# Feed-forward of a two-layer encoder trunk: both down blocks of a pair stand between its seventh and its third product

## The chip, the cores and the metric

The kernel runs on one core of a Trainium2 chip. The metric is the device time of one execution in microseconds (us). A difference of 0.2% is 2.9 us here.

## What is computed

Two layers over 512 tokens of width 1024, all in float32. Each layer has a mixer (attention in layer 0, an mLSTM in layer 1), a cross-attention to a memory, and a gated feed-forward; the change lies in the feed-forward of both layers:

```
def conv_ffn(xn, w_up, conv_w, conv_b, w_down):
    h = causal_depthwise_conv(xn @ w_up, conv_w) + conv_b     # 1024 -> 2 x 2816, 3 taps
    g, u = jnp.split(h, 2, axis=-1)
    return (jax.nn.gelu(g) * u) @ w_down                      # 2816 -> 1024
...
x = x + conv_ffn(rms_norm(x, ffn_norm[layer]), ffn_w_up[layer], ffn_conv_w[layer], ffn_conv_b[layer], ffn_w_down[layer])
```

## The kernel before

The 2816 columns of each half are worked through in 22 "pairs" p of 128 columns of g and the 128 columns of u that belong to them. Activations lie transposed, so that a product has a 128x128 piece of a weight as the stationary operand and 256 or 512 tokens as the moving one. For precision every float32 operand is split into a high and a low part, and each product is done as three matmuls (high x high, low x high, high x low: lines 292, 293, 294, in `mm3`). Splitting a weight costs ScalarE (ACT) one cast to the high part and VectorE (DVE) one subtraction to the low part (line 283, `sub`).

Pair 0 goes the plain way (`plain`). Pairs 1 to 21 (`seven`) use a scheme of seven half-size products instead of eight, each of 12 matmuls with 256 moving columns, in the order p1, p5, p6, p2, p7, p3, p4 of the code (the "seventh" product is p7, the "third" p3, the "last" p4 in the code's names). Their stationary operands are sums of weight blocks:

- f3 (raw tile `raw`) serves p1 and p2, f1 (raw tile `sa`, summed by a POOL transfer that accumulates) serves p5 and p7; both are 1024 columns wide and lie in three rotating slots `wh`/`wl`, which they share with the down blocks.
- `s2` serves p6, `s4` serves p3, `a22` serves p4: 512 columns each, one slot each. Both `s2` and `s4` are made from the tile `sb` (lines 1768 and 1774).

Between the products, results are passed on: after p1 ACT seeds a second PSUM bank with its negative (line 1801, "v"); after p5 ACT copies a bank to `u5`, after p6 to `u2` (line 1805). p7 writes on to the bank that `u2` is copied from, so it waits for that copy. After p7 DVE forms one quarter of the result (`hs<-acc,u`, line 1808), after p3 another (`hs<-s,u`, line 1808), after p2 and p4 ACT copies the other two (lines 1818 and 1825). When all four are there, DVE scales them by the norm (line 1831), and a "tail" follows: two convolution starts on ACT (1684), four taps on DVE (1691), GELU on ACT (1699), the product with u on DVE (1701), and the split of the activation (1705 on ACT, `al` on DVE).

The products with `w_down` ("down blocks") run over chunks of 2 or 4 pairs, 8 blocks per chunk. A block is 6 or 12 matmuls with 512 moving columns into a bank `w`; its weight comes through the tile `dr` (two slots; cast on line 1568, subtraction on 283). For most blocks ACT first seeds the bank with the sum so far (1598) and copies it back afterwards (1855). Where a block is followed by a 256-column product, the last 128 columns of its low part are written with an offset, which makes its subtraction two instructions. From pair 3 on, a call of `fill()` in the code of a pair takes the next block from a queue and puts it at that place.

The order on every engine is set by a list scheduler (`Sched`) with the given due times and costs, and from there it is fixed: each engine works its own queue in order and waits at the head of it.

Of the kernel before, what the change touches and what calls it, by code (L numbers as in the profile page):

```python
# [66 lines left out]
class Plan:  # L67
# [11 lines left out]
    def add(self, fn, dur=0.0, deps=(), prio=None, take=(), free=(), chain=(), pre=(), after=0.0, order=(), load=(), st=None):  # L79
        it = Item(fn, dur, [d for d in deps if d is not None], len(self.items) if prio is None else prio, take, free, chain, pre, after, order, load, st)  # L80
        it.n = len(self.items)
        self.items.append(it)
        return it
# [154 lines left out]
class Builder:  # L238
# [22 lines left out]
    def bank(self, tag):  # L261
        tag, bufs = BANKS[tag]
        return self.til(self.aux, tag, bufs=bufs)
# [1257 lines left out]
    def ffn_steps(self, layer, mp):  # L1521
# [15 lines left out]
        def pe(dur, fn, deps, take=(), free=()):  # L1537
            clock[0] += dur
            return add("PE", dur, fn, deps, clock[0] - dur, take, free, 0.2)
# [198 lines left out]
        def seven(p, fill):  # L1738
# [41 lines left out]
            def product(s, c, xh, xl, bank, first):  # L1780

                for k in range(4):
                    w = slice(c + k * P, c + (k + 1) * P)
                    self.mm3(st[bank][:, :256], s["wh"][:, w], s["wl"][:, w], xh(k), xl(k), first and k == 0, k == 3, True)
# [22 lines left out]
            def less(out, a, b):  # L1807
                tt_(out=out(), in0=a(), in1=b(), op=ALU.subtract)
# [10 lines left out]
            p7 = pe(n, lambda: product(f1, 0, *T3, "Y", False), [u2, p5], (), [("h", f1)])  # L1819
            c22 = add("DVE", 0.34, lambda: less(hs(1, 1), bank("Y"), lambda: st["u5"][:]), [p7, u5, get], clock[0], (), [("u5", bu5)])  # L1820
            fill()
            p3 = pe(n, lambda: product(s4, 0, *X(1, 1), "R", False), [u5, w4], (), [("s4", s4)])
            c12 = add("DVE", 0.34, lambda: less(hs(0, 1), bank("R"), lambda: st["u2"][:]), [p3, u2, get], clock[0], (), [("s", br), ("u2", bu2)])
            p4 = pe(n, lambda: product(a22, 0, *T4, "Y", False), [c22, w22], (), [("a22", a22)])
# [6 lines left out]
                tt_(out=h, in0=h, in1=self.rb.unsqueeze(1).to_broadcast([P, 2, 512]), op=ALU.mult)  # L1831

            m = add("DVE", 1.14, scaled, [c11, c22, c21, c12, normed], clock[0] + 2.0)
            fill()
            tail(p, st, [[m], [m]], clock[0] + 3.0)


# [3 lines left out]
        def down(c, m, steps=1):  # L1841
            first, nk = CHUNKS[c]
            onto = (self.x[m], [xadded[m]]) if c < LAST and (c, m) not in ((0, 0), (0, 1)) else None
            d, last = block(
                t[f"down{c}"][layer, m], nk, lambda k: tuple(a[:] for a in acts[first + k]), clock[0], "w", [acted[first + k] for k in range(nk)], steps,
                "dr" if c < LAST else "raw", OFF, onto,
            )
            last.block, d["step"] = d, 16
            if m == 7:
                for k in range(nk):  # L1850
                    joined([last], last.prio, [("act", acted[first + k].st)])
            if onto is None:
                e = add("DVE", 0.6, lambda: self.xadd(m, d["ps"]), [last, xadded[m], *formed], clock[0] + 3.0, (), [("w", d)])
            else:
                e = add("ACT", act(512), lambda: nc.scalar.copy(self.x[m][:], d["ps"][:]), [last, *formed], clock[0] + 1.0, (), [("w", d)])
            xadded[m] = e
            return e

        def fill():
            nonlocal queue  # L1860
            if queue:
                down(*queue.pop(0))
# [468 lines left out]
```

## Time and profile before

| | us |
|---|---|
| median of 3 runs | 1452.01 (1451.99 to 1452.08) |
| the profiled execution, its own time | 1451.94 |
| its span in the trace | 1450.1 |
| TensorE (PE) busy | 1435.6 |
| DVE busy | 1226.5 |
| ACT busy | 1009.8 |
| POOL busy | 74.8 |

The time of the execution and its span differ by 1.84 us, which lie around the span. The feed-forward of layer 0 stands at about 415 to 739 us of the span, that of layer 1 at about 1114 to 1436. In a row of the timeline the first number is the start in us from the span's start, the second the duration, then engine, line, operation, output and inputs; in brackets the idle time before it and what ended it. Instructions of one engine overlap a little: what counts in a queue is the distance from start to start.

### The profile page before, as it was taken

Reading aid. Unit: us, or ns where it says so; the run is one execution under the profiler, and the core shown is the slowest. Engines: PE = TensorE matmul, PEld = TensorE weight load, DVE = VectorE, ACT = ScalarE, POOL = GpSimd, SP = SyncE. Lnnn points to the kernel's source line nnn. Section 1 sums busy time; section 2 is a strip of 40 time slices with the busy share of each in tenths; the row PEclk is TensorE's granted clock in tenths of the full one; section 3 lists DMA queues with packets and bytes.
Section 4 is the critical chain, followed back from the end, with each engine's and each line's share of the span. In section 5 each row is a group of like instructions: output and inputs, shape, how many; then the busy total and the mean of one; then the engine's idle time right before and its main releaser. Section 6 shows DMA issues by size and latency. Waiting matters only on the chain.

```text
span 1450.1 us, 24100 instructions
## 1 busy us (share of the span) xinstructions
PE 1435.6 (99%) x8971; PEld 1274.2 (88%) x8971; DVE 1226.5 (85%) x2199; ACT 1009.8 (70%) x1830; POOL 74.8 (5%) x116
## 2 busy tenths in 40 slices
PE   9999999999999999999999999999999999999998
PEld 7888788998889999999888788889988999999997
DVE  7789987877899988888689888887779999888875
ACT  7689766655678777777657676566566787777775
POOL 0001120000000000000000100000000000000000
PEclk9999999999999999999999999999999999999999
DMA  5222337652246665552233322656313666655312
GB/s 199 89 74 73 110 119 214 178 167 87 95 118 170 183 164 158 155 166 68 66 128 106 121 94 98 188 144 181 132 52 113 165 182 175 153 163 159 101 52 95
DMA packets 73367, 190.38 MB, mean 131 GB/s; under 512 B 8081, under 2 KB 10258, under 8 KB 73250
## 3 DMA queue, kind: packets, MB, share of 16 engines
q1 hardware_dynamic: 65474, 162.30, 33.6%
q0 software_dynamic: 7200, 26.22, 10.6%
q8 instruction: 70, 1.15, 0.3%
q14 instruction: 47, 0.39, 0.1%
q10 hardware_dynamic: 576, 0.33, 0.1%
HBM read 186.69 MB, written 2.13 MB: 130 GB/s over the span
## 4 chain that ended last, share of the span: by engine, by line
PE 80%; DVE 12%; ACT 4%; issue 2%; DMA 1%; POOL 0%; SPq 0%; DVEq 0%; ACTq 0%; POOLq 0%
PE acc L292 14%; PE acc L293 14%; PE acc L294 14%; PE w L294 6%; PE w L292 6%; PE w L293 6%; PE s L294 3%; PE s L292 3%; PE s L293 3%; DVE wl L283 3%; PE acc L353 2%; PE acc L355 2%; PE acc L354 2%; DVE c L1691 1%; DVE x L774 1%
## 5 line engine op out<-in xcount | busy, mean ns | idle before, releaser
L283 DVE TENSOR_TENSOR wl<-raw,wh 128x1024 fp32r<-128x1024 f32 (+2 forms) x181 | 209.4, 1157 | 37.5 <-ACT wh L286 29.0
L292 PE MATMUL acc<-xh,wh 128*128 128x256 f32 (+1 forms) x624 | 206.9, 332 | 0.2 <-ACT v L1932 0.2
L294 PE MATMUL acc<-xh,wl 128*128 128x256 f32 (+1 forms) x624 | 205.6, 329 | 0.1
L293 PE MATMUL acc<-xl,wh 128*128 128x256 f32 (+1 forms) x624 | 205.5, 329 | 0.0
L286 ACT CAST wh<-raw 128x1024 fp32r<-128x1024 f32 (+1 forms) x123 | 124.8, 1019 | 73.3 <-PE acc L293 35.7
L1691 DVE SCALAR_TENSOR_TENSOR c<-hs,vec,c 128x512 f32<-128x512 f32 x176 | 131.0, 747 | 14.6 <-ACT c L1684 12.6
L292 PEld LDWEIGHTS acc<-xh,wh 128*128 128x128 f32 x624 | 117.2, 188 | 12.8 <-ACT v L1932 0.9
L293 PEld LDWEIGHTS acc<-xl,wh 128*128 128x128 f32 x624 | 117.2, 188 | 12.2
L294 PEld LDWEIGHTS acc<-xh,wl 128*128 128x128 f32 x624 | 117.1, 188 | 12.1 <-DVE wl L283 0.7
L294 PE MATMUL w<-ah,wl 128*128 128x512 f32 x320 | 125.3, 392 | 0.0
L293 PE MATMUL w<-al,wh 128*128 128x512 f32 x320 | 124.8, 390 | 0.0
L292 PE MATMUL w<-ah,wh 128*128 128x512 f32 x320 | 124.8, 390 | 0.0
L1684 ACT ACTIVATE c<-hs,vec 128x512 f32<-128x512 f32 x88 | 71.2, 816 | 13.8 <-DVE hs L1831 7.4
L283 DVE TENSOR_TENSOR wl<-sa,wh 128x1024 fp32r<-128x1024 f32 x52 | 63.5, 1221 | 20.2 <-ACT wh L1762 18.5
L1568 ACT CAST wh<-dr 128x512 fp32r<-128x512 f32 (+1 forms) x80 | 46.0, 575 | 42.1 <-PE w L293 35.3
L294 PEld LDWEIGHTS w<-ah,wl 128*128 128x128 f32 x320 | 60.1, 188 | 12.7
L1762 ACT CAST wh<-sa 128x1024 fp32r<-128x1024 f32 x42 | 44.0, 1049 | 36.3 <-PE w L293 33.3
L292 PEld LDWEIGHTS w<-ah,wh 128*128 128x128 f32 x320 | 60.1, 188 | 10.3 <-ACT w L1598 0.2
L293 PEld LDWEIGHTS w<-al,wh 128*128 128x128 f32 x320 | 60.1, 188 | 10.1
L283 DVE TENSOR_TENSOR wl<-dr,wh 128x128 fp32r<-128x128 f32 (+3 forms) x148 | 55.6, 410 | 9.4 <-ACT wh L1568 9.3
L1747 POOL DMA_DIRECT2D sa<-in_up_dram x42 | 35.9, 855 | 514.8 <-DVE hs L1831 209.7
L283 DVE TENSOR_TENSOR s<-sb,s 128x512 fp32r<-128x512 f32 x88 | 60.2, 685 | 2.2
(571 smaller groups left out, 4656.1 us busy)
## 6 DMA issues: line engine op xcount, KB each, us to landing
raw<-in_up_dram SPq DMA_DIRECT2D x46, 512.0 KB, 3.2
sa<-in_up_dram SPq DMA_DIRECT2D x42, 512.0 KB, 3.4
sa<-in_up_dram POOLq DMA_DIRECT2D x42, 512.0 KB, 5.8
dr<-in_down_dram SPq DMA_DIRECT2D x64, 256.0 KB, 2.6
ra<-in_up_dram SPq DMA_DIRECT2D x42, 256.0 KB, 2.8
raw<-in_xk_dram SPq DMA_DIRECT2D x16, 512.0 KB, 3.3
raw<-in_wo_dram SPq DMA_DIRECT2D x16, 512.0 KB, 3.8
raw<-in_xv_dram SPq DMA_DIRECT2D x16, 512.0 KB, 3.3
```

What stands on the lines that cost most here:

```text
L283: self.nc.vector.tensor_tensor(out=lo, in0=v, in1=hi.bitcast(F32), op=ALU.subtract)
L286: self.nc.scalar.copy(hi, v)
L292: mm(out, wh, xh, start=first, stop=False, skip_group_check=parts)
L293: mm(out, wh, xl, start=False, stop=False, skip_group_check=parts)
L294: mm(out, wl, xh, start=False, stop=last, skip_group_check=parts)
L353: mm(ps, xh[k][:, ts], wh[:, ws], start=(k == 0), stop=False)
L354: mm(ps, xh[k][:, ts], wl[:, ws], start=False, stop=False)
L1568: nc.scalar.copy(st["wh"][:, :cols], st[tag][:, :cols])
L1684: nc.scalar.activation(st["c_"][:, j, :], hs()[:, j, 2:514], AF.Identity, scale=self.col("cw", (layer * 3 + 2) * 44 + blk), bias=self.col( ...
L1691: nc.vector.scalar_tensor_tensor(out=c, in0=hs()[:, j, n : n + 512], scalar=w, in1=c, op0=ALU.mult, op1=ALU.add)
L1747: return add("POOL", 0.0029 * cols, lambda: nc.gpsimd.dma_start(out(), src(), accum_op=ALU.add), deps, due, (), (), 6.0)
L1762: nc.scalar.copy(s["wh"][:, :cols], raw())
```

## The change

One call of `fill()` is moved within `seven`: before, one down block came between p7 and p3 and one after p4; now both come between p7 and p3, and none after p4. The number of matmuls, casts and transfers is the same.

```
             p7 = pe(n, lambda: product(f1, 0, *T3, "Y", False), [u2, p5], (), [("h", f1)])
             c22 = add("DVE", 0.34, lambda: less(hs(1, 1), bank("Y"), lambda: st["u5"][:]), [p7, u5, get], clock[0], (), [("u5", bu5)])
             fill()
+            fill()
             p3 = pe(n, lambda: product(s4, 0, *X(1, 1), "R", False), [u5, w4], (), [("s4", s4)])
...
             m = add("DVE", 1.14, scaled, [c11, c22, c21, c12, normed], clock[0] + 2.0)
-            fill()
             tail(p, st, [[m], [m]], clock[0] + 3.0)
```

Lines behind the first of these places move down by one (1825 becomes 1826, 1831 becomes 1832). The scheduler answers with another order on the engines. On ACT, in a pair in the middle of layer 0, from the seed after p1 (line 1801) to the copy after p2 (1818), before:

```order
L1801 ACTIVATE acc_1272_6808<-acc_1266_6772 128x256
L1598 COPY w_6805<-x_143 128x512
L1684 ACTIVATE c_6770<-hs_4591,vec 128x512
L1805 COPY u_1273_6825<-s_6792 128x256
L1699 ACTIVATE c_6770<-c_6770 128x512
L1805 COPY u_1275_6843<-acc_1272_6808 128x256
L1762 CAST s_1276_6846<-sb_6585 128x512
L1705 CAST ah_6881<-c_6770 128x512
L1568 CAST wh_6861<-dr_6703 128x512
L1818 COPY hs_4590<-acc_1266_6772 128x256
```

The same stretch in the changed kernel (`u<-s` is the copy to u5, `u<-acc` the copy to u2, `s<-sb` the cast of the next pair's s2):

```order
L1801 ACTIVATE acc_1271_6796<-acc_1267_6763 128x256
L1684 ACTIVATE c_6812<-hs_4591,vec 128x512
L1805 COPY u_1274_6815<-s_6782 128x256
L1684 ACTIVATE c_6812<-hs_4591,vec 128x512
L1762 CAST s_1275_6830<-sb_6598 128x512
L1805 COPY u_1276_6832<-acc_1271_6796 128x256
L1699 ACTIVATE c_6812<-c_6812 128x512
L1568 CAST wh_6848<-dr_6690 128x512
L1818 COPY hs_4590<-acc_1267_6763 128x256
```

Both convolution starts and the cast of s2 now stand ahead of the copy to u2. ACT rows in this order stand in pair 6 and in pairs 8 to 19 of each layer.

At the end of a pair, between the cast of f1 (`wh<-sa`) and the copy after p4, ACT had this before:

```order
L1762 CAST wh_6905<-sa_6387 128x1024
L1855 COPY x_142<-w_6745 128x512
L1598 COPY w_6926<-x_144 128x512
L1762 CAST s_1287_6924<-sb_6585 128x512
L1762 CAST a_1290_6944<-ra_6604 128x512
L1825 COPY hs_4590<-acc_1272_6808 128x256
```

and has this now (`wh<-dr` is the cast of the next pair's first down block, which takes the slot of the second block):

```order
L1762 CAST wh_6891<-sa_6379 128x1024
L1855 COPY x_142<-w_6721 128x512
L1598 COPY w_6901<-x_144 128x512
L1568 CAST wh_6916<-dr_6760 128x512
L1855 COPY x_143<-w_6743 128x512
L1598 COPY w_6923<-x_145 128x512
L1762 CAST s_1292_6938<-sb_6598 128x512
L1762 CAST a_1295_6956<-ra_6618 128x512
L1826 COPY hs_4590<-acc_1271_6796 128x256
```

Copy and seed of the second block moved ahead of the cast of s4 (`s<-sb`).

On DVE, in pair 4 of layer 0, from the result after p7 (`hs<-acc,u`) to the subtraction for f1 of pair 5 (`wl<-sa`), before:

```order
L1808 TENSOR_TENSOR hs01_4591<-acc2_1019_5175,u5_1028_5231 128x256
L1691 SCALAR_TENSOR_TENSOR c_1032_5253<-hs00_4590,vec_103,c_1032_5253 128x512
L283 TENSOR_TENSOR s2_1024_5210<-sb_1006_5106,s2_1024_5210 128x512
L1691 SCALAR_TENSOR_TENSOR c_1032_5253<-hs00_4590,vec_103,c_1032_5253 128x512
L1808 TENSOR_TENSOR hs01_4591<-s_1023_5197,u2_1025_5213 128x256
L283 TENSOR_TENSOR wl_1036_5277<-raw_967_4815,wh_1035_5276 128x1024
L1691 SCALAR_TENSOR_TENSOR c_1032_5253<-hs00_4590,vec_103,c_1032_5253 128x512
L1774 TENSOR_TENSOR sb_1006_5106<-sb_1006_5106,raw_967_4815 128x512
L1691 SCALAR_TENSOR_TENSOR c_1032_5253<-hs00_4590,vec_103,c_1032_5253 128x512
L283 TENSOR_TENSOR wl_1039_5311<-sa_974_4871,wh_1038_5310 128x1024
L1701 TENSOR_TENSOR c_1032_5253<-c_1032_5253 128x512
```

and now:

```order
L1808 TENSOR_TENSOR hs01_4591<-acc2_1019_5175,u5_1028_5232 128x256
L1691 SCALAR_TENSOR_TENSOR c_1032_5253<-hs00_4590,vec_103,c_1032_5253 128x512
L283 TENSOR_TENSOR wl_1035_5261<-raw_967_4815,wh_1034_5260 128x1024
L1691 SCALAR_TENSOR_TENSOR c_1032_5253<-hs00_4590,vec_103,c_1032_5253 128x512
L1774 TENSOR_TENSOR sb_1007_5108<-sb_1007_5108,raw_967_4815 128x512
L1691 SCALAR_TENSOR_TENSOR c_1032_5253<-hs00_4590,vec_103,c_1032_5253 128x512
L1808 TENSOR_TENSOR hs01_4591<-s_1023_5197,u2_1025_5213 128x256
L1701 TENSOR_TENSOR c_1032_5253<-c_1032_5253 128x512
L283 TENSOR_TENSOR wl_1039_5304<-sa_974_4871,wh_1038_5303 128x1024
```

The tail's product of pair 3 (1701) now stands ahead of f1's subtraction, and the subtraction of s2 has gone up, out of this stretch.

On PE both blocks stand together in pairs 5 to 18 and in pair 20 of each layer, between p7 and p3; in pair 4 they stand together between p3 and p4. In pair 3 both come after p4, as before; in pair 21 the one block that it has stays between p7 and p3. The transfers on SP's queue are the same ones; in a pair the load of one `dr` now goes out ahead of the load of `ra`, where it came behind it.

More of the change, by code (lines that the diff above doesn't have):

```diff
@@ L1821, in seven @@
             fill()
+            fill()
             p3 = pe(n, lambda: product(s4, 0, *X(1, 1), "R", False), [u5, w4], (), [("s4", s4)])
@@ L1833, in seven @@
             m = add("DVE", 1.14, scaled, [c11, c22, c21, c12, normed], clock[0] + 2.0)
-            fill()
             tail(p, st, [[m], [m]], clock[0] + 3.0)
```

## The prediction

> **What bounds the kernel now.** I read the page first, then a table of engine times by stage, then the timeline of PE, ACT and DVE in single pairs. From the page, the busy shares and the shares of the chain that ended last:
>
> ```profile
> PE 1435.6 (99%) x8971; PEld 1274.2 (88%) x8971; DVE 1226.5 (85%) x2199; ACT 1009.8 (70%) x1830; POOL 74.8 (5%) x116
> PE 80%; DVE 12%; ACT 4%; issue 2%; DMA 1%; POOL 0%; SPq 0%; DVEq 0%; ACTq 0%; POOLq 0%
> ```
>
> PE is busy for 99% of the span. Moving blocks removes no matmul, so a gain can come only from the little time in which PE doesn't stream, and a loss only from waits that it is made to take. The stages of the feed-forward differ (pairs 3 and 4, pairs 5 to 8 and pairs 13 to 16 of layer 0, then pairs 5 to 8 of layer 1; behind the stretch its length, then the busy times, with the number of instructions, of PE, its weight loads, DVE, ACT and POOL, then the granted clock, 1.00 throughout, and the transfers):
>
> ```profile
> 432.00:462.00 30.00, 29.18 (x229) 27.77 (x227) 30.00 (x50) 23.37 (x44) 1.70 (x2) 1.00 0.61 165
> 462.00:521.00 59.00, 58.84 (x438) 55.36 (x437) 57.33 (x94) 47.62 (x91) 4.28 (x5) 1.00 0.69 183
> 584.00:644.00 60.00, 60.00 (x433) 56.13 (x432) 52.39 (x81) 43.65 (x81) 3.44 (x4) 1.00 0.58 158
> 1160.00:1220.00 60.00, 60.00 (x448) 56.39 (x447) 58.31 (x95) 48.67 (x93) 4.28 (x5) 1.00 0.66 182
> ```
>
> In the early pairs DVE is full (30.00 of 30.00 us, 57.33 of 59.00) and PE waits now and then; in the middle pairs DVE has 7.6 of 60 us free and PE is never idle. So there are two regimes, and the change has to be priced in each.
>
> **Part 1: edges on PE.** Starts of a middle pair: the last two matmuls of a block, the first of p1 behind it, of p5 and p7, then of the block behind p7, of p3, p4 and the next block.
>
> ```profile
> 590.99 0.39 PE L293 MATMUL w<-al,wh 128*128 128x512 f32 x1
> 591.21 0.40 PE L294 MATMUL w<-ah,wl 128*128 128x512 f32 x1
> 591.45 0.28 PE L292 MATMUL acc<-xh,wh 128*128 128x256 f32 x1
> 592.83 0.28 PE L292 MATMUL s<-kv,wh 128*128 128x256 f32 x1
> 596.91 0.28 PE L292 MATMUL acc<-kv,wh 128*128 128x256 f32 x1
> 598.27 0.39 PE L292 MATMUL w<-ah,wh 128*128 128x512 f32 x1
> ...
> 601.01 0.28 PE L292 MATMUL s<-xh,s 128*128 128x256 f32 x1
> 602.39 0.28 PE L292 MATMUL acc<-kv,a 128*128 128x256 f32 x1
> 603.75 0.39 PE L292 MATMUL w<-ah,wh 128*128 128x512 f32 x1
> ```
>
> A product behind a product takes 1.36 us (602.39 to 603.75), a product behind a block 1.38 (591.45 to 592.83, 601.01 to 602.39). The way out of a block is seen at its last matmul as well: 590.99 to 591.21 is 0.22 or 0.23 in these rounded starts, 591.21 to 591.45 is 0.24. For the way in I take 0.01, by what is left of the block's 2.74 us (598.27 to 601.01) over 12 such steps; that is my estimate, at the limit of the rounding. With two blocks together, one of the two ways out of a block and one of the ways in are gone: 0.02 + 0.01 = 0.03 us a pair. Sixteen pairs of each layer change (4 to 18 and 20), so 32 x 0.03 = -1.0 us. PE has no cover, so this counts in full where PE streams; the bounds are -0.5 (only the 0.02 of p1, on 24 pairs) and -1.1.
>
> **Part 2: the middle pairs.** The moved block needs its weight earlier: its cast waits until p2 gives back f3's slot, and p7 and the first block (1.36 + 2.74 us) cover it, against p7, a block, p3 and p4 before. Cast 0.62, subtraction 0.76: covered. The load of `dr` for it is one of these:
>
> ```profile
> dr<-in_down_dram SPq DMA_DIRECT2D x64, 256.0 KB, 2.6
> ```
>
> Its slot comes free with the subtraction for the block two places earlier, most of a pair (15.04 us, 591.45 to 603.75 + 2.74) ahead of its own cast, so 2.6 us to landing stay hidden, also behind the load of `ra`, which the other `dr` has now passed. The tighter place is p7. It writes on to the bank that ACT copies to u2, and in the changed order that copy stands behind two convolution starts and a cast. Pair 7 of layer 0 has this order already today (the scaling on DVE, then on ACT the first convolution start, the cast of s2 and the u2 copy; the copy to u5 and the second convolution start are left out):
>
> ```profile
> 487.52 1.21 DVE L1831 TENSOR_TENSOR hs<-hs,rb 128x1024 f32<-128x1024 f32 x1
> ...
> 488.76 0.82 ACT L1684 ACTIVATE c<-hs,vec 128x512 f32<-128x512 f32 x1 [0.34 <-DVE hs L1831]
> ...
> 490.47 0.62 ACT L1762 CAST s<-sb 128x512 fp32r<-128x512 f32 x1
> 490.99 0.36 ACT L1805 COPY u<-acc 128x256 f32<-128x256 f32 x1
> ```
>
> From the start of the scaling to the end of the u2 copy: 490.99 + 0.36 - 487.52 = 3.83 us. And pair 6 shows what happens when that ends late (the copy, then the weight load of p7):
>
> ```profile
> 479.01 0.36 ACT L1805 COPY u<-acc 128x256 f32<-128x256 f32 x1
> 479.42 0.19 PEld L292 LDWEIGHTS acc<-kv,wh 128*128 128x128 f32 x1 [0.19 <-ACT u L1805]
> ```
>
> The load starts 0.05 after the copy's end (479.37). So p7 can go 3.88 us after the scaling starts. When does the scaling start now? The chain at the end of a pair, today:
>
> ```profile
> 600.97 1.05 ACT L1762 CAST wh<-sa 128x1024 fp32r<-128x1024 f32 x1 [1.46 <-PE w L293]
> 601.93 0.58 ACT L1855 COPY x<-w 128x512 f32<-128x512 f32 x1
> 602.54 0.59 ACT L1598 COPY w<-x 128x512 f32<-128x512 f32 x1
> 603.07 0.62 ACT L1762 CAST s<-sb 128x512 fp32r<-128x512 f32 x1
> 603.95 0.62 ACT L1762 CAST a<-ra 128x512 fp32r<-128x512 f32 x1 [0.26 <-PE acc L294]
> ...
> 603.72 0.69 DVE L283 TENSOR_TENSOR s<-sb,s 128x512 fp32r<-128x512 f32 x1
> 604.45 0.69 DVE L1768 TENSOR_TENSOR sb<-sa,raw 128x512 f32<-128x512 f32 x1
> 605.06 0.68 DVE L283 TENSOR_TENSOR a<-ra,a 128x512 fp32r<-128x512 f32 x1
> 605.66 1.22 DVE L1831 TENSOR_TENSOR hs<-hs,rb 128x1024 f32<-128x1024 f32 x1
> ```
>
> These clock times can serve for the changed kernel: a block ends ahead of p3 at 601.01 in both, and p4 ends at 603.75, where now p1 of the next pair begins. In the new order the cast that waits for the block is that of a down block, 0.53 from start to start (the distance of a 512-column cast to the row behind it, 490.47 to 490.99, with 0.01 to spare) instead of 0.96. So: 600.97 + 0.53 + 0.61 (copy to seed) + 0.53 (seed to cast) = 602.64 for the cast of s4, + 0.65 = 603.29 for its subtraction, + 0.73 = 604.02, + 0.61 = 604.63 for a22's, + 0.60 = 605.23 for the scaling. By the other branch (a22's cast waits for p4) it is 603.95 + 0.62 + 0.03 + 0.60 = 605.20. p7 may load at 605.23 + 3.88 = 609.11. PE wants it 5.44 after p1 (596.91 - 591.45, less the edge of 0.02) less 0.11 for the load's lead, at 603.75 + 5.44 - 0.11 = 609.08. It comes 0.03 late. Before, the u2 copy had no cast ahead of it and p7 had a wide margin. Pairs 8 to 19 of both layers have the order: 24 x 0.03 = +0.7 us. Bounds: 0, by the second branch, and +2.4, if every link together is 0.07 longer than here (the spread of the starts that I see is 0.01 to 0.03 a link).
>
> **Part 3: the early pairs.** The DVE row for pair 5's f1, the tail's product that follows it, and two waits of PE:
>
> ```profile
> 461.09 1.21 DVE L283 TENSOR_TENSOR wl<-sa,wh 128x1024 fp32r<-128x1024 f32 x1
> 462.22 0.67 DVE L1701 TENSOR_TENSOR c<-c 128x512 f32<-128x512 f32 x1
> ...
> 462.35 0.19 PEld L294 LDWEIGHTS s<-kv,wl 128*128 128x128 f32 x1 [0.35 <-DVE wl L283]
> 475.29 0.19 PEld L294 LDWEIGHTS s<-kv,wl 128*128 128x128 f32 x1 [0.17 <-DVE wl L283]
> ```
>
> DVE works without a pause here, so a place in its queue is a time. The new order puts the product of line 1701 (0.60 from start to start, as the 512-column rows at 605.06 and 605.66) ahead of f1's subtraction; a merged subtraction of a block gives a little back. f1 is ready some 0.5 later, and p5 of pair 5 waits for it already: 0.35 becomes 0.85 to 0.95. Until pair 8 DVE has hardly any free time to give this back (1.67 of 59 us), and the waits of pair 6 (0.17, 0.19) hang on the same queue. I take +0.5 us a layer, +1.0 in all; bounds 0 (all given back, the blocks' own subtractions being due later) and +2.2 (pair 6 loses as much again).
>
> **Sum** against the execution's own time: 1451.94 - 1.0 + 0.7 + 1.0 = 1452.64. The median of the runs is 0.07 above that execution, so **1452.7 us**. Less than 0.2% (2.9 us, about what a measurement can tell from no change) either way is "same": 1449.1 to 1454.9.
>
> **Rivals.**
> - *Slower, by p7.* If the chain of part 2 is longer than I reckon by 0.10 us or more, 24 pairs lose more than 2.4 us beyond the 0.7, and the verdict changes. One way: if a DVE instruction could start only where the row ahead of it ends. Then 604.02 + 0.69 + 0.68 = 605.39 for the scaling, 0.16 later, and 24 x 0.19 = 4.6 instead of 0.7 gives 1456.6. For it speaks that the margin is nil; against it that the rows show starts at 0.60 behind a start of 0.68 (605.06, 605.66). Chance 0.20 for this rival, in whatever link. [...]
> - *Gain.* With two blocks in a row, ACT and DVE have 5.5 us without a new demand, and the early waits vanish: 0.35 + 0.17 + 0.19 = 0.71 a layer, 1.4 in all, if layer 1 waits as much. With the edges and without parts 2 and 3: 1452.0 - 1.0 - 1.4 = 1449.6. Against it: DVE's total stays, and its queue is what PE waits for. Chance 0.16, a quarter of it beyond 0.2%.
> - *Transfers.* The load of `dr` comes late behind a blocked `ra`: a wait of up to 2.6 us at a block, but most of a pair of lead stands against it. If each of 30 pairs lost only 0.2 us: 1458. Chance 0.04, half of it within 0.2%.
>
> **The numbers.** My forecast holds 0.60, within 1451.4 to 1454.9. Faster: 0.04. Same: 0.60 + 0.12 + 0.02 = 0.74. Slower: 0.20 + 0.02 = 0.22. The range goes from all edges gained and no loss (1452.0 - 1.1 = 1450.9) to parts 2 and 3 at their upper bounds with the smaller gain (1452.0 - 0.5 + 2.4 + 2.2 = 1456.1): 1450.8 to 1456.2.
>
> **What would show it.** In the trace after: p1 to p1 of a middle pair at 15.04 - 0.03 + 0.03 = 15.04 us, with a wait for the u2 copy of some hundredths in front of p7, and none in front of a block; in front of pair 5's p5 a wait of about 0.9 us for f1's subtraction. Wrong would be: waits for transfers, a period under 15.01 or over 15.15, or waits of PE in the last pairs, where I expect none.

## The result, and the profile after

The changed kernel takes 1453.92 us (median of 21 runs, 1453.26 to 1454.62) against 1452.01 us before: a ratio of 1.0014, 95% interval 1.0008 to 1.0020. That is 1.9 us slower, inside the 0.2% that I called "same"; forecast were 1452.7 us and a range of 1450.8 to 1456.2. The profiled execution took 1454.55 us, 0.63 over its median; a second profiled execution (the last experiment) took 1453.65.

From the page of the changed kernel, then the stages that were shown of before, in the same columns:

```profile
PE 1436.0 (99%) x8971; PEld 1275.3 (88%) x8971; DVE 1217.6 (84%) x2167; ACT 1013.3 (70%) x1830; POOL 74.9 (5%) x116
PE 79%; DVE 12%; ACT 4%; issue 3%; DMA 1%; POOL 0%; SPq 0%; DVEq 0%; ACTq 0%; POOLq 0%
```

```profile
432.00:462.00 30.00, 29.20 (x228) 27.72 (x226) 29.96 (x50) 22.91 (x44) 1.70 (x2) 1.00 0.65 170
462.00:521.00 59.00, 57.90 (x432) 54.57 (x432) 54.79 (x85) 46.84 (x88) 4.27 (x5) 1.00 0.66 181
584.00:644.00 60.00, 60.00 (x431) 56.08 (x431) 50.62 (x77) 44.17 (x80) 3.44 (x4) 1.00 0.59 157
1160.00:1220.00 60.00, 58.87 (x440) 55.42 (x439) 56.71 (x89) 47.75 (x90) 3.84 (x5) 1.00 0.64 179
```

These shares tell little: DVE has 32 instructions fewer (2167 against 2199), since blocks that are followed by a block need no second piece in their subtraction. PE, though, has lost time in the early pairs (57.90 busy of 59 us, 58.84 before; 58.87 of 60 in layer 1, 60.00 before). In the middle stretch it is busy for all of 60.00 us and still does two matmuls fewer (431, 433 before). A busy share doesn't show that loss; the starts of p1 do. The first p1 of pair 8 and of pair 19, in both layers:

```profile
501.83 0.28 PE L292 MATMUL acc<-xh,wh 128*128 128x256 f32 x1
667.70 0.28 PE L292 MATMUL acc<-xh,wh 128*128 128x256 f32 x1
1202.57 0.28 PE L292 MATMUL acc<-xh,wh 128*128 128x256 f32 x1
1368.23 0.28 PE L292 MATMUL acc<-xh,wh 128*128 128x256 f32 x1
```

(667.70 - 501.83) / 11 = 15.079, and 15.060 in layer 1; before it was 15.040 in both. All stretches, by the same starts (us, layer 0 / layer 1):

| from p1 to p1 | before | after | after, second execution |
|---|---|---|---|
| pairs 4 to 7 together | 53.43 / 53.38 | 54.14 / 54.16 | 54.13 / 54.19 |
| mean of pairs 8 to 18 | 15.040 / 15.040 | 15.079 / 15.060 | 15.037 / 15.050 |
| pair 19 | 8.18 / 8.18 | 8.62 / 8.71 | 8.63 / 8.62 |
| pair 20 | 16.38 / 16.38 | 16.36 / 16.67 | 16.36 / 16.36 |
| pair 21, to the first block behind p4 | 12.46 / 12.48 | 12.28 / 12.28 | 12.28 / 12.28 |

**A middle pair.** The chain that part 2 reckoned, in pair 14 of the changed kernel (DVE, then ACT, then p7's first weight load):

```profile
593.18 0.69 DVE L283 TENSOR_TENSOR a<-ra,a 128x512 fp32r<-128x512 f32 x1
593.78 1.22 DVE L1832 TENSOR_TENSOR hs<-hs,rb 128x1024 f32<-128x1024 f32 x1
...
595.03 0.81 ACT L1684 ACTIVATE c<-hs,vec 128x512 f32<-128x512 f32 x1 [0.81 <-DVE hs L1832]
...
596.73 0.61 ACT L1762 CAST s<-sb 128x512 fp32r<-128x512 f32 x1
597.24 0.37 ACT L1805 COPY u<-acc 128x256 f32<-128x256 f32 x1
...
597.65 0.19 PEld L292 LDWEIGHTS acc<-kv,wh 128*128 128x128 f32 x1
```

From the scaling to the end of the copy: 597.24 + 0.37 - 593.78 = 3.83, as forecast; p7 loads 3.87 after the scaling (forecast 3.88). The matmuls around it:

```profile
597.63 0.28 PE L294 MATMUL acc<-xh,wl 128*128 128x256 f32 x1
597.74 0.30 PE L292 MATMUL acc<-kv,wh 128*128 128x256 f32 x1
597.88 0.28 PE L293 MATMUL acc<-kv,wh 128*128 128x256 f32 x1
...
599.17 0.39 PE L292 MATMUL w<-ah,wh 128*128 128x512 f32 x1
...
604.66 0.28 PE L292 MATMUL s<-xh,s 128*128 128x256 f32 x1
```

p7's first step is 0.14 instead of 0.11 (597.74 to 597.88): there is the lateness of 0.03. But the 11 steps behind it take 1.29, 0.117 each, where p2's take 0.113; and the 24 steps of the two blocks take 5.49, where they take 5.46 in experiment one. Being 0.03 late cost this pair 0.10. No row bracket shows it: the trace names no wait here.

**Pair 19** has another order ahead of p7. With no further down block to prepare, the cast at the end of pair 18 is one of f3, 1024 columns wide:

```profile
664.93 1.05 ACT L1762 CAST wh<-raw 128x1024 fp32r<-128x1024 f32 x1 [0.28 <-PE w L293]
...
667.02 0.62 ACT L1762 CAST s<-sb 128x512 fp32r<-128x512 f32 x1
...
673.06 0.37 ACT L1805 COPY u<-acc 128x256 f32<-128x256 f32 x1
```

```profile
673.03 0.28 PE L294 MATMUL acc<-xh,wl 128*128 128x256 f32 x1
673.48 0.38 PE L292 MATMUL acc<-kv,wh 128*128 128x256 f32 x1 [0.17 <-ACT u L1805]
673.70 0.28 PE L293 MATMUL acc<-kv,wh 128*128 128x256 f32 x1
...
673.47 0.19 PEld L292 LDWEIGHTS acc<-kv,wh 128*128 128x128 f32 x1 [0.37 <-ACT u L1805]
```

p7 starts 0.45 behind the last matmul of p2 instead of 0.11, so 0.34 late, and its own first step takes 0.22 instead of 0.11: 0.45 lost, which is the 0.44 of the table (0.46 against experiment one, where this pair takes 8.16). The brackets show 0.17 of it at the matmul and 0.37 at its weight load.

**Pair 5.** The tail's product and f1's subtraction on DVE, and p5's third weight load; below it the first weight load of p7 in pair 6:

```profile
461.05 0.68 DVE L1701 TENSOR_TENSOR c<-c 128x512 f32<-128x512 f32 x1
461.65 1.21 DVE L283 TENSOR_TENSOR wl<-sa,wh 128x1024 fp32r<-128x1024 f32 x1
...
462.91 0.19 PEld L294 LDWEIGHTS s<-kv,wl 128*128 128x128 f32 x1 [1.09 <-DVE wl L283]
...
479.53 0.19 PEld L292 LDWEIGHTS acc<-kv,wh 128*128 128x128 f32 x1 [0.41 <-ACT u L1805]
```

The wait for f1 is 1.09 (0.35 before; forecast 0.85 to 0.95), and p7 of pair 6 waits 0.41 for the u2 copy (0.19 before). p7 of pair 7, which did not wait before, is about 0.26 late as well.

### The profile page after: what moved, and what is told of

It reads as the page before. It is cut to its first block, busy times and chain, and to the rows that moved or that the text cites. A ratio compares the mean times of both kernels' runs of the same rounds, so it can differ in the third digit from the quotient of the medians.

```text
span 1452.8 us, 23993 instructions
## 1 busy us (share of the span) xinstructions
PE 1436.0 (99%) x8971; PEld 1275.3 (88%) x8971; DVE 1217.6 (84%) x2167; ACT 1013.3 (70%) x1830; POOL 74.9 (5%) x116
## 4 chain that ended last, share of the span: by engine, by line
PE 79%; DVE 12%; ACT 4%; issue 3%; DMA 1%; POOL 0%; SPq 0%; DVEq 0%; ACTq 0%; POOLq 0%
PE acc L292 14%; PE acc L293 14%; PE acc L294 14%; PE w L292 6%; PE w L293 6%; PE w L294 6%; PE s L294 3%; PE s L292 3%; PE s L293 3%; DVE wl L283 2%; PE acc L353 2%; PE acc L355 2%; PE acc L354 2%; DVE c L1691 1%; DVE cv L1962 1%
## 5 line engine op out<-in xcount | busy, mean ns | idle before, releaser
L292 PE MATMUL acc<-mem,wh 128*128 128x256 f32 (+1 forms) x192 | 61.6, 321 | 0.0
L293 PE MATMUL acc<-mem,wh 128*128 128x256 f32 (+1 forms) x192 | 61.0, 318 | 0.0
```

What stands on the lines that cost most here:

```text
L292: mm(out, wh, xh, start=first, stop=False, skip_group_check=parts)
L293: mm(out, wh, xl, start=False, stop=False, skip_group_check=parts)
```

## The experiments

The first four, on one chip, against a kernel before of 1452.82 us there. The 95% intervals of the ratios are about 0.0009 wide to either side, 1.3 us, so the times alone decide little between neighbouring theories; the starts of p1 decide. **One:** in pairs 8 to 19 the cast of s2 is planned behind the u2 copy, so that ACT does the copy first.

```
-            w2 = split(s2, 512, [b2], at, ...
+            w2 = split(s2, 512, [b2] + [u for q, u in kept2 if q == p - 1 and 8 <= q <= 19], at, ...
             u2 = add("ACT", act(256), lambda: kept("u2", "Y"), [p6], clock[0], [("u2", bu2)])
+            kept2.append((p, u2))
```

> The changed kernel, with one ACT order altered in pairs 8 to 19 of each layer: the copy to u2 goes ahead of the cast of the next pair's s2, so it ends some 0.5 us earlier. Theory A (a start of p7 that is 0.02 us late costs about 0.09, because PE's steps behind it are 0.1175 instead of 0.1134 us until the blocks have let the weight loads run ahead; the saved edges are real): no wait before p7, the period of the middle pairs falls from 15.03-15.10 to 15.01, pair 19 loses nothing, time 1451.6 us. Theory B (the longer period comes from the two blocks standing together, not from the copy): period stays 15.07 to 15.10, only the 0.17 wait of pair 19 goes, time 1453.3 to 1453.9.

1452.67 us, ratio 1.0000 (0.9991 to 1.0009). The period is 15.000 in both layers, pair 19 takes 8.16. The u2 copy, p7's first weight load and first matmul, and the p1 of this pair and the next:

```profile
596.32 0.36 ACT L1805 COPY u<-acc 128x256 f32<-128x256 f32 x1
...
597.22 0.19 PEld L292 LDWEIGHTS acc<-kv,wh 128*128 128x128 f32 x1
...
597.33 0.28 PE L292 MATMUL acc<-kv,wh 128*128 128x256 f32 x1
...
591.89 0.28 PE L292 MATMUL acc<-xh,wh 128*128 128x256 f32 x1
606.89 0.28 PE L292 MATMUL acc<-xh,wh 128*128 128x256 f32 x1
```

The copy ends at 596.68, 0.54 ahead of the load. So the edges give 0.04 a pair (15.040 to 15.000; I had 0.03), and the late copy took it back, 0.06 to 0.08 a pair in the first execution of the changed kernel. Theory B falls. The time was 1 us over theory A's 1451.6, but the kernel before was 0.8 over its usual median on this chip too.

**Two to four:** one part of the change alone.

```
             fill()
-            fill()
+            if p >= 8:      # "middle"; p < 8 in "early"
+                fill()
...
+            if not (p >= 8):
+                fill()
             tail(p, st, [[m], [m]], clock[0] + 3.0)
```

> The change in pairs 8 to 21 alone; pairs 3 to 7 keep the order of before. Theory A (the parts are separate: about +0.75 us a layer from pairs 4 to 7, the rest from pairs 8 to 20): the 0.89 wait for f1 goes, time 1453.9 - 1.5 = 1452.4 us, middle period as in the changed kernel. Rival (the early waits are given back later, DVE having free time from pair 8 on): 1453.5 to 1453.9.

1452.80 us, ratio 0.9999 (0.9990 to 1.0007). Pairs 4 to 7 take 53.44 / 53.45 again, pairs 8 to 18 15.035, pair 19 8.61. The early loss is gone and that of the late copy is still there, as theory A has it.

> The change in pairs 3 to 7 alone; pairs 8 to 21 keep the order of before. Theory A: time 1452.0 + 1.5 = 1453.5 us, with the 0.89 wait for f1 in pair 5 and waits for u2 in pairs 6 and 7, and a middle period of 15.04. Rival (given back later): 1452.0 to 1452.5.

1454.35 us, 1.0011 (1.0002 to 1.0020): +1.5 as theory A has it. Pairs 4 to 7 take 54.16 / 53.76, pair 19 8.18. In layer 1 pair 3 took 12.55, 12.19 in layer 0, and pair 5 was shorter by as much, so pairs 3 to 7 together are the better measure: 66.35 / 66.31 here, 66.34 / 66.33 in the changed kernel, 65.62 / 65.63 before. The early loss isn't given back later: pairs 8 and 9 take 15.06 to 15.15, and from pair 10 on the period is 15.04.

> The change in pairs 8 to 21 alone, with the copy to u2 ahead of the cast of s2 in pairs 8 to 19. Theory A: what is left of the change are its saved edges, 26 x 0.03 = 0.8 us less, and about 0.2 a layer in pair 21: 1450.9 us, a version ahead of both kernels. Theory B (the blocks together cost by themselves): 1452.0 or more.

1451.49 us, 0.9990 (0.9981 to 0.9999): 1.3 less than before. Within the intervals the parts add up: +1.5 for the early pairs and 0 for the middle ones, against +1.9 for both; and -1.3 for the middle ones without the late copy.

The next four, on a chip where before took 1452.18 us. **Five:** `at + 7.0` of the tail's product becomes `at + 17.0` for p = 3.

> The changed kernel; only the due time of the tail's product (line 1701) of pair 3 is 10 later, so that f1's subtraction of pair 5 stands ahead of it on DVE again. Theory A (that product is what makes f1 late): the wait of 0.89 in pair 5 falls to about 0.35, pairs 4 to 7 get 0.5 us a layer shorter, time 1 us under the changed kernel, about +0.9 us against before. Rival (DVE is full and the place doesn't matter, what is put later makes something else late by as much): the wait turns up elsewhere in pairs 5 to 7, and the time stays at +1.9.

1453.66 us, 1.0010 (1.0001 to 1.0019), +1.5. f1's subtraction and p5's third load, then the load of p7 in pair 7:

```profile
460.25 1.21 DVE L283 TENSOR_TENSOR wl<-sa,wh 128x1024 fp32r<-128x1024 f32 x1
...
461.51 0.19 PEld L294 LDWEIGHTS s<-kv,wl 128*128 128x128 f32 x1
...
491.01 0.19 PEld L292 LDWEIGHTS acc<-kv,wh 128*128 128x128 f32 x1 [0.67 <-ACT u L1805]
```

In layer 0 the wait for f1 (1.09 in the changed kernel) has no bracket any more, though the load still comes only 0.05 behind the end of the subtraction (461.46); in layer 1 a wait of 0.48 for f1 stays (1.10 in the changed kernel). A wait of 0.67 for the u2 copy stands in pair 7. Pairs 4 to 7 take 53.41 / 53.81, but in layer 0 pair 3 took 12.55 again: pairs 3 to 7 together take 65.96 / 65.99, 0.38 and 0.35 less than in the changed kernel, where theory A has 0.5. So line 1701's product does make f1 late; and part of what it gives turns up as the next wait, as the rival has it.

**Six:** both blocks of pairs 8 to 21 behind p4 (the `fill()` between p7 and p3 left out there, two ahead of `tail`).

> The order of before, but in pairs 8 to 21 both blocks come after the last product, none between p7 and p3. Theory A (the gain is in the edge that two blocks in a row save, wherever they stand): period 15.00 if no copy is late, 26 x 0.04 = 1.0 us under before. Rival (p7 is tight here too, since the copy to u2 now stands behind a GELU, a split and the cast of s2): a wait in front of p7, p3 or p4 in each pair, period 15.1 or more, 1.5 us or more over before.

1454.40 us, 1.0017 (1.0008 to 1.0026). From p1 to p1 of a middle pair, then the load of p4 in pair 8:

```profile
590.97 0.28 PE L292 MATMUL acc<-xh,wh 128*128 128x256 f32 x1
605.97 0.28 PE L292 MATMUL acc<-xh,wh 128*128 128x256 f32 x1
...
508.81 0.19 PEld L292 LDWEIGHTS acc<-kv,a 128*128 128x128 f32 x1 [0.73 <-DVE hs L1808]
```

From pair 10 or 11 on the middle pairs run at 15.00 here too: the edge gain doesn't depend on the place, and p7 isn't tight. The loss stands in pair 8 (15.88, in layer 1 15.83), where p4 waits for DVE to read out p7's bank and no block covers that, in pair 9 (15.11 / 15.39) and in pair 19 (9.89 / 9.95 to the next p1, 8.18 before; pair 20 gives 0.75 of it back). Neither theory had this, and why the pairs between don't wait is not shown.

**Seven and eight** add an ACT copy of the same bank behind the u2 copy in pairs 8 to 19: to the changed kernel, and to the kernel of experiment one.

```
                 nc.scalar.copy(st[tag][:], bank(n_)())
+                if tag == "u2" and 8 <= p <= 19:
+                    for i in range(2 - 1):
+                        nc.scalar.copy(st["Y"][:, 256 + 128 * i : 512], st["Y"][:, 128 * i : 256])
```

> The changed kernel with one more ACT copy of 256 columns from p7's bank to unused columns of the same bank, right behind the copy to u2 in pairs 8 to 19; p7 waits for it too. It needs about 0.25 us from start to start, so p7 is 0.27 late instead of 0.02. Theory A (a late start costs its own length and then the slower steps behind it, as in pair 19: 0.34 late, 0.46 lost): period 15.35 to 15.40. Rival (only a very small lateness brings the slow steps, a longer one lets the weight loads recover): 15.27. Time 1453.9 + 24 x 0.19 to 0.32 = 1458.5 to 1461.6 us.

1460.50 us, 1.0058 (1.0046 to 1.0071), a period of 15.31. The extra copy, p7's first load, and the matmuls:

```profile
613.58 0.38 ACT L1808 COPY acc<-acc 128x256 f32<-128x256 f32 x1
...
614.01 0.19 PEld L292 LDWEIGHTS acc<-kv,wh 128*128 128x128 f32 x1 [0.22 <-ACT acc L1808]
...
613.71 0.28 PE L294 MATMUL acc<-xh,wl 128*128 128x256 f32 x1
614.01 0.38 PE L292 MATMUL acc<-kv,wh 128*128 128x256 f32 x1
614.23 0.28 PE L293 MATMUL acc<-kv,wh 128*128 128x256 f32 x1
614.34 0.28 PE L294 MATMUL acc<-kv,wl 128*128 128x256 f32 x1
...
615.48 0.39 PE L292 MATMUL w<-ah,wh 128*128 128x512 f32 x1
```

Without a wait p7's load would start with p2's last matmul, at 613.71 (as at 597.22 against 597.33 in experiment one, a load stands one step of 0.11 ahead of its own matmul). It starts at 614.01, 0.30 late. The matmul starts together with it, the step behind takes 0.22, and the remaining 11 take 1.25, 0.114 each: no slow steps in this pair. The mean loss is 0.31, the lateness of the load: that is the rival's size (its 15.27 was for a lateness of 0.27), and theory A's surcharge does not show. But slow steps are not kept to the very small lateness, as the rival has it: in 6 of the 22 pairs 8 to 18 the last ten steps of p7 take 0.118, and these pairs take 15.33 where the others take 15.29 to 15.31.

> The same extra copy in the kernel that has the copy to u2 ahead of the cast of s2. Theory A (only the lateness at p7 counts, the ACT work itself is free): the bank is free 0.2 us before p7 wants it, period 15.00, time as without the extra copy (-0.15 us against before). Rival (the extra ACT work delays the conversions behind it): period 15.05 or more.

1452.69 us, 1.0003 (0.9995 to 1.0012), period 15.000: the extra ACT work is free as long as p7 isn't late. In pair 19, where the extra copy makes p7's load 0.21 late, the pair takes 8.37 / 8.47 instead of 8.16, and pair 20 of layer 1 takes 16.66 instead of 16.36.

**Nine to eleven,** where before took 1452.46 us: the diff of one with 6 <= q, then with 7 <= q together with five, then the kernel of experiment four (the change in pairs 8 to 21 with the copy first) once more.

> The changed kernel, with the copy to u2 ahead of the cast of s2 in pairs 6 and 7 as well as 8 to 19. Theory A (in pairs 6 and 7 too the copy is what p7 waits for, 0.3 to 0.5 us each with the step behind the wait): pairs 4 to 7 of each layer 0.7 us shorter than in the changed kernel, 1.4 us less than with pairs 8 to 19 alone, that is about -1.5 us against before. Rival (DVE is full until pair 8; what p7 gains there is lost in the next wait): pairs 4 to 7 as long as in the changed kernel, about -0.15 us.

1451.05 us, 0.9992 (0.9983 to 1.0001), -1.4. Pairs 4 to 7 take 53.59 / 53.69, 0.55 and 0.47 less than in the changed kernel. It comes from pair 6, where p7's load was 0.48 late in the changed kernel and is on time here. In pair 7 the copy stands first as well, but the load stays about 0.3 late: there ACT waits 0.51 for DVE's scaling ahead of the convolution starts.

> Both alterations of the order at once: the tail's product of pair 3 due later (f1 of pair 5 ahead of it) and the copy to u2 ahead of the cast of s2 in pairs 7 to 19. From the single ones: +1.5 (f1 alone) - 2 x 0.5 (the wait of 0.47 in pair 7) - 22 x 0.07 (middle pairs) - 2 x 0.45 (pairs 19 and 20) = -1.9 us against before. Rival (given back in the pairs where DVE is full): -0.5.

1450.57 us, 0.9989 (0.9980 to 0.9997): -1.9 as added up from the single ones. Pairs 4 to 7 take 53.37 / 52.87, pairs 3 to 7 (pair 3 of layer 1 took 12.55) 65.56 / 65.43. This keeps the change in all pairs and beats both kernels.

> The kernel with the change in pairs 8 to 21 alone and the copy to u2 first, once more beside these two: -1.1 us by the edges of 26 pairs (0.04 each), -1.3 as measured before; period 15.00.

1450.95 us, 0.9989 (0.9980 to 0.9998), -1.5.

**Twelve:** the changed kernel once more, for one profile.

> The changed kernel itself in another profiled execution. Theory A (how many of PE's steps behind a start that is some 0.02 us late are slow is a matter of the single execution): the mean period of pairs 8 to 18 comes out anywhere from 15.035, as with the change in pairs 8 to 21 alone, to 15.08, and the slow products of pair 20 in layer 1 may be gone (16.36 for that pair). Rival (it belongs to the kernel's order): 15.08 and 15.06 in the two layers again, and 16.67 for pair 20 of layer 1.

1453.65 us, one before beside it 1452.05. The table above has its stretches: 15.037 and 15.050 in the middle, 16.36 for pair 20 of layer 1. Theory A holds: the order is the same, and whether PE's steps turn slow behind a late start differs between executions (last section). Pairs 4 to 7 and pair 19 came out the same within 0.1.

## Why the prediction was right, and which terms were mis-sized

The sign, the class and the range held; the sizes did not: +0.7 us was forecast and +1.9 measured. "Same" is a band of 2.9 us to either side, so that it held says little about the terms. Every loss of the sum came out about twice as large or more, and gains that the sum did not have took part of that back, which was luck. By parts, forecast and then measured in the first profile of after, which is 2.61 over the profile of before:

| | forecast | measured |
|---|---|---|
| edges of pairs 8 to 18, both layers | 22 x -0.03 = -0.66 | 22 x -0.04 = -0.88 |
| p7 of pairs 8 to 18 | 22 x 0.03 = +0.66 | +0.65 + 0.88 = +1.53 (second execution +0.96) |
| pairs 19 and 20 | 0.0 | +0.44 + 0.53 - 0.02 + 0.29 = +1.24 (second +0.85) |
| pairs 4 to 7 with their edges | +1.0 - 0.24 = +0.76 | +0.71 + 0.78 = +1.49 |
| pair 21 | 0 | -0.18 - 0.20 = -0.38 |
| the rest of the span | 0 | -0.39 |

- **Edges (part 1).** Right in kind, 0.04 instead of 0.03; too small was the way into a block, taken as 0.01: two blocks apart take 2 x 2.74, in a row 5.46 (experiment one), so it is about 0.02. That the edges come from blocks in a row and not from the place between p7 and p3 is shown by experiments one and six.
- **p7 (part 2).** The chain came out to 0.01 us, the lateness too. The mis-sized step is "24 x 0.03": it takes a late load to cost its lateness. That is nearly so for 0.30 (experiment seven, 0.31), for 0.44 (pair 19 of layer 0, 0.46) and for 0.02 to 0.03 in experiment two (0.035), where PE's steps stayed at 0.113. Where they turned slow behind the late load, 0.02 to 0.03 cost 0.05 to 0.10, and pair 19 of layer 1 with pair 20 lost 0.86 by a load 0.46 late (8.71 + 16.67 against 8.16 + 16.36).
- **Pair 19.** The error is in "pairs 8 to 19 of both layers have the order": I priced them all by one middle pair. In pair 19 the cast at the end of the pair before is f3's, 0.43 longer in this chain, and the load 0.44 late (673.47 against 673.03). With the copy first this pair takes 8.16. The prediction named waits in the last pairs as a sign of being wrong; this is one.
- **Early pairs (part 3).** f1's wait came as reckoned, somewhat larger (1.09). What was left out: the longer wait for u2 at p7 of pair 6 and the new one in pair 7, whose ACT order has the cast of s2 ahead of the copy too. Putting the copy first took 0.5 a layer off in pair 6 and nothing in pair 7 (experiment nine).
- **Pair 21.** I expected nothing in the last pairs. There was a wait of before that I hadn't seen, since no bracket names it: p6 starts 0.18 behind the start of p5's last matmul, where 0.11 is usual, and then takes a step of 0.22. It starts 0.05 behind the end of ACT's seed after p1 (693.96), which ran 2.38 behind p1's start; in the changed kernel the seed runs 1.56 behind it, and the wait is gone.

```profile
693.59 0.37 ACT L1801 ACTIVATE acc<-acc 128x256 f32<-128x256 f32 x1
...
693.83 0.28 PE L294 MATMUL s<-kv,wl 128*128 128x256 f32 x1
694.01 0.38 PE L292 MATMUL acc<-kv,s 128*128 128x256 f32 x1
694.23 0.28 PE L293 MATMUL acc<-kv,s 128*128 128x256 f32 x1
```

- **Rivals.** The one by p7 named the right place, but not the size: DVE's scaling starts 0.60 behind the row ahead of it (593.18 to 593.78), whose record lasts 0.69. A start at that row's recorded end, the rival's one way, would have been 0.09 later (593.87); the trace does not show that. Early waits grew instead of vanishing, so the gain didn't come. No weight load of the feed-forward's PE stream waits for a transfer in the list of waits.

## What to carry to other kernels

When PE never idles, read the starts, not the busy share, and price a moved step by what then stands ahead of the instruction that PE waits for on the other engines: here one cast ahead of a 256-column copy cost the middle pairs all that the change gave them, 0.04 us a pair. Price the odd pair at the end of a loop by its own rows. The change alone lost 1.9 us; with two places in the other engines' order put right (f1's subtraction on DVE, the copy to u2 on ACT) it gained 1.9.

## What the runs showed of the hardware

What a wait costs is read at the weight load, not in the bracket: a load that starts 0.30 or 0.44 late costs PE 0.31 or 0.46 where its steps stay at 0.113, of which the brackets of the matmul and the load show 0.17 to 0.37. In the stream a product's load starts one step of 0.11 before its own matmul (597.22 against 597.33 in experiment one); after the wait in experiment seven both start together (614.01), and the next step is twice as long (0.22, to 614.23).

A load that is late by 0.02 to 0.03 has no such double step: in the changed kernel's pair 14 it is 0.14 (597.74 to 597.88). But behind a late load, slightly late or more, PE's steps are in some cases 0.118 instead of 0.113 up to the next block. Of the 22 pairs 8 to 18 of both layers, 16 have such steps in the first execution of the changed kernel (they are the ones that take 15.05 to 15.10), 9 in the second, none in experiment two, and 6 in experiment seven with its lateness of 0.30. The longest stretch of the first execution begins in pair 19 of layer 1, whose p7 loads 0.46 late: it goes on through p3 and the six products from pair 20's p1 to its blocks, at 1.41 or 1.42 each instead of 1.36. Pair 3's 12.55 in some runs is the same, behind a long wait in pair 2: in layer 0 of experiment eleven, pair 2's p4 starts 1.09 behind the matmul ahead of it (432.38 to 433.47), the steps behind it are 0.118, and pair 3 takes 12.54. p7's load of pair 19, then the first two products of pair 20:

```profile
1374.01 0.19 PEld L292 LDWEIGHTS acc<-kv,wh 128*128 128x128 f32 x1 [0.38 <-ACT u L1805]
...
1376.94 0.28 PE L292 MATMUL acc<-xh,wh 128*128 128x256 f32 x1
...
1378.36 0.28 PE L292 MATMUL s<-kv,wh 128*128 128x256 f32 x1
```

In the second execution of the same kernel pair 19 is 0.45 late again and nothing of this follows. What turns the steps slow in one execution and not in the other is open; the granted clock is 1.00 in the middle stages of both layers and in this pair.
